# A list schedule of the MLP with other landing times, and six instead of four prepared weights ahead of its last part

## The chip, the cores and the metric

The kernel runs on one core of one Trainium2 chip. The metric is the device time of one execution in microseconds (us). The engines of the core are TensorE (PE; its weight loads are shown apart as PEld), VectorE (DVE), ScalarE (ACT), GpSimd (POOL) and SyncE (SP). SP issues plain transfers; POOL issues the transfers that add what they bring to what is there.

## The reference, cut to what matters

The model is an encoder of two layers on 512 tokens of width 1024. Each layer has a token part (attention, retention, gates) and a channel part, and the change is in the channel part alone:

```python
for i in range(DEPTH):
    ...
    x = layer_norm(DEEPNORM_ALPHA * x + y, ln1_g[i], ln1_b[i])
    ffn = conv_glu_ffn(x, w_up[i], conv_w[i], conv_b[i], w_down[i])
    ple = jax.nn.sigmoid(x @ w_ple_gate[i]) * (p[i] @ w_ple_proj[i])
    x = layer_norm(DEEPNORM_ALPHA * x + ffn + ple, ln2_g[i], ln2_b[i])

def conv_glu_ffn(x, w_up, conv_w, conv_b, w_down):
    h = x @ w_up
    hp = jnp.pad(h, ((0, 0), (1, 1), (0, 0)))
    h = hp[:, :-2] * conv_w[0] + hp[:, 1:-1] * conv_w[1] + hp[:, 2:] * conv_w[2] + conv_b
    a, b = jnp.split(h, 2, axis=-1)
    return (jax.nn.gelu(a) * b) @ w_down
```

Everything is float32. The up projection makes 2 x 2816 columns, the down projection takes 2816 back to 1024.

## The kernel before, in words

**Split operands.** A matmul here takes a float32 operand as a sum of a high part and a low part. ACT casts a weight to its high part (hi), DVE subtracts to get the low part (lo), and PE does three matmuls for each product (`mm3`: hi with hi, hi with lo, lo with hi). One weight is a tile of 128 x 1024, so it costs one load, one cast on ACT and one subtraction on DVE before PE can use it.

**Seven products for eight.** The larger matrix products are done block by block in seven products named a, c, t1, t2, d, t3 and t4, as in Strassen's scheme. Their weights are sums of blocks. Four of them are a chain in one buffer: a is loaded, split, then POOL adds a block to the same buffer (an accumulating transfer), which makes the raw t1; that is split, POOL adds again for t2, and again for t4. So t2's weights can't be split before t1's are, plus the time of the added transfer. t3 is a load and one added block; c and d are plain loads. Each product has two weights (j = 0 and 1).

**Segments.** The 22 row blocks of the hidden layer are cut into three segments of 3, 4 and 4 pairs (`SEGS`). For each segment an up part makes the hidden tiles and a down part multiplies them into the residual sum R. In the first segment the second weight of each down product is half as wide (512), since it has three pairs.

**What sets the order.** The engines run their instructions in the order in which the program issues them. Up to the first segment's up part, and again from the last down part on, that order comes from `Stream.get`, which prepares weights a few items ahead as it hands them out. In between, in `region` (lines 1615 to 1908), a list scheduler decides: `Plan` collects jobs for PE ("P"), ACT ("A"), DVE ("V"), POOL ("G") and SP ("S"), each with a duration from `COST`, the jobs it must follow, the buffers it takes and a due time. `dues` works the due times backwards from PE's fixed order. For a job with a transfer it subtracts the transfer and `COST["land"]`. `order` then plays the engines forward: whenever one is free it starts the most urgent job whose predecessors are done, whose buffers are free and whose due time is no further off than its `early`. A transfer counts as done at the end of a shared pipe plus `COST["land"]`. `run` does this for six settings (`PLANS`), keeps the one in which PE ends first, and issues the jobs in that order.

**Buffers in the plan.** `CAP` counts units ("u", 26), pairs for split weights ("w", 3), raw buffers ("r", 3), PSUM banks ("b") and temporaries ("t"). A weight with a pool of its own takes two units for its pair.

**The start of the region.** Some weights are already split there, some are only loaded or are being added to (`it.raw is not None`, line 1625). For the latter the plan holds their buffer and takes their data as landed at a fixed time, by `pl.past(6.0)` in line 1628. `TAIL` says when ACT and DVE are done with what was issued before (lines 217, 1867, 1896).

**The end of the region.** Lines 1877 to 1890 add the first four weights of the last down part (a and c, two each) to the plan, with due times counted from the plan's end `pl.now`, and the added blocks that follow them. Line 1905 then tells the stream that four weights are prepared. The last down part (from line 1912) takes them with `ws.get()`, which prepares t1, t2, d, t3 and t4 as it goes. At its first product the first layer also loads the next layer's input p (`ple_in`); the last layer loads the constants of the final norm (`ln_consts`).

The functions named in the steps below are `Stream.get` (534), `Plan.dues` (136), `Plan.order` (146) and `region` (1615) with `raw_of`, `plus` and `weights`.

Of the kernel before, what the change touches and what calls it, by code (L numbers as in the profile page):

```python
# [35 lines left out]
SEGS = (3, 4, 4)  # L36
# [36 lines left out]
DOWN = ("a", "c", "t1", "t2", "d", "t3", "t4")  # L73
CAP = {"u": 26, "w": 3, "r": 3, "b": 4, "t": 6}
COST = {"hi": 1.05, "lo": 1.22, "neg": 1.06, "centre": 0.79, "taps": 1.5, "gelu": 0.65, "mul": 0.69, "into": 0.69,
        "copy": 0.62, "issue": 1.0, "load": 1.45, "add": 3.0, "land": 3.0}
EARLY = {"w": 14, "g": 13, "s": 15, "c": 13, "d": 13, "t3": 14, "a": 28, "t1": 38, "t2": 30, "t4": 18}
AHEAD = 14

# [134 lines left out]
PLANS = ((1.0, 0), (0.9, 0), (0.8, 0), (1.0, 2), (0.6, 0), (1.2, 3))  # L214
SOON = 5
NEAR, SPARE = 10, 0
TAIL = (3.6, 4.3)
VG_HELD = (('0t1', '1t1', '0t2', '0c', '1t2', '1a', '1d', '1t3'), ('0a', '0c', '0t1', '1t1', '1t3', '1t2', '0t3', '0t2', '1d'))


# [42 lines left out]
def _f(a):  # L263
    return a.bitcast(F32)


def trunk(tc, wpack, x_nat, x_tr, head, p_tr, rpb, decay, ln_par, ln_col, conv, cos_t, sin_t, dist, xi_d, zd, mask, ident_d, out):
# [4 lines left out]
    with ExitStack() as es:  # L272
        pool = lambda name, bufs, **k: es.enter_context(tc.tile_pool(name=name, bufs=bufs, **k))
        cp = pool("const", 1)
        up = pool("unit", N_UNIT)
# [280 lines left out]
        ws = Stream()  # L556
# [261 lines left out]
        for l in range(DEPTH):  # L818
# [796 lines left out]
            def region():  # L1615

                pl = Plan(CAP)
                seq, at = ws.seq, [ws.nget]
                have, raws, ops, far = {}, {}, {}, []
                for it in seq[ws.nget:ws.nget + 40]:  # L1620
                    if it.hl is not None:
                        b = pl.held(*(("w", 1) if it.pool is None else ("u", 2)))
                        b.tile = it.hl
                        have[it] = b, None, None
                    elif it.raw is not None:
                        b = pl.held("r" if it.own is False or it.kind in "cdwgs" else "u")
                        b.tile = it.raw
                        raws[it] = b, pl.past(6.0)

                def raw_of(it):  # L1630

                    if it in raws:
                        return raws[it]
                    ll, c, o, w = it.src
                    raw = Buf(("u",) if it.own else ("r",), 1, lambda p: (up if p == "u" else rp).tile([P, 1024], F32, tag="u" if p == "u" else "raw", name=nm("raw")))
                    ok = pl.add("S", 0.1, lambda: nc.sync.dma_start(raw.tile[:, :w], wpack[ll, c][:, o:o + w]), takes=[raw],
                                dma=COST["load"] * w / 1024, early=EARLY[it.kind] - 4 + (AHEAD if it.plus else 0))
                    if it.plus is not None:
                        ok = plus(it, raw, [ok])
                    return raw, ok  # L1640

                def plus(it, raw, after):

                    ll, c, o, w = it.plus
                    return pl.add("G", COST["issue"], lambda: nc.gpsimd.dma_start(raw.tile[:, :w], wpack[ll, c][:, o:o + w], accum_op=ALU.add),
                                  after, uses=[raw], dma=COST["add"] * w / 1024)
# [4 lines left out]
                def weights(it, pools=None):  # L1651

                    if it in have:
                        return have[it]
                    hl = Buf(pools or (("u",) if it.kind in ("a", "t1", "t2", "s") else ("w", "u")), 2, pair)
                    if it.kind == "s":
                        ll, c, o, w = it.src
                        hi = pl.add("G", COST["issue"], lambda: nc.gpsimd.dma_start(hl.tile[0], wpack[ll, c]), takes=[hl], dma=COST["load"], early=EARLY["s"])
                        neg = pl.add("A", COST["neg"], lambda: nc.scalar.activation(hl.tile[1], _f(hl.tile[0]), AF.Copy, scale=-1.0), [hi], uses=[hl])
                        lo = pl.add("G", COST["issue"], lambda: nc.gpsimd.dma_start(hl.tile[1], wpack[ll, c], accum_op=ALU.add), [neg], uses=[hl], dma=COST["add"])  # L1660
                        have[it] = hl, hi, lo
                        return have[it]
                    raw, ok = raw_of(it)
                    cs, f = slice(0, it.width), it.width / 1024
                    hi = pl.add("A", COST["hi"] * f, lambda: nc.scalar.copy(hl.tile[0][:, cs], raw.tile[:, cs]), [ok], takes=[hl], uses=[raw], early=EARLY[it.kind])
                    lo = pl.add("V", COST["lo"] * f, lambda: nc.vector.tensor_sub(hl.tile[1][:, cs], raw.tile[:, cs], _f(hl.tile[0][:, cs])), [hi], uses=[raw, hl])
                    if it.nxt is not None:
                        raws[it.nxt] = raw, plus(it.nxt, raw, [hi, lo])
                    have[it] = hl, hi, lo
                    return have[it]  # L1670
# [192 lines left out]
                for p in range(SEGS[0]):  # L1863
                    halves[p // 2].tile = a11p[p // 2]
                    ops[0, p, 0] = halves[p // 2], (lambda p=p: a11[p]), []
                    b = pl.held("u")
                    ops[0, p, 1] = b, (lambda p=p: k2[p]), [pl.past(TAIL[1])] if p == p2 else []
                    for i in range(2):
# [4 lines left out]
                for s in range(1, len(SEGS)):  # L1873
                    up_part(s)
                    if s < len(SEGS) - 1:
                        down(s)
                s, nxt = len(SEGS) - 1, seq[at[0]:at[0] + 4]
                keep = []
                for i, it in enumerate(nxt):
                    hl, hi, lo = weights(it, ("w",) if it.pool is None else ("u",))  # L1880
                    lo.due = pl.now + 2.72 * i - 1
                    keep.append(hl)
                    hl.left += 1
                    if it.nxt is not None:
                        raws[it.nxt][0].left += 1
                        raws[it.nxt][1].due = pl.now + 2
                    if it.early is not None:
                        raws[it.early] = raw_of(it.early)
                        raws[it.early][0].left += 1
                        raws[it.early][1].due = pl.now + 6  # L1890
                for p in range(SEGS[s]):
                    for f, due in ((0, 0), (1, 5), (2, 10), (3, 10)):
                        b, _, js = ops[s, p, f]
                        b.left += 1
                        js[-1].due = min(js[-1].due, pl.now + due)
                pl.run({"A": TAIL[0], "V": TAIL[1]})
                for it in nxt:
# [4 lines left out]
                for p in range(SEGS[s]):  # L1902
                    a11[p], k2[p] = ops[s, p, 0][1](), ops[s, p, 1][1]()
                    sa[p], sb[p] = ops[s, p, 2][1](), ops[s, p, 3][1]()
                ws.nget, ws.nprep = at[0], at[0] + 4
                ws.nload = ws.nprep
                while seq[ws.nload].src is None or seq[ws.nload].kind == "t3":
                    ws.nload += 1

            region()  # L1910
            tile = NF
            for s in (len(SEGS) - 1,):
# [191 lines left out]
                for k in BOUND if not last else ("t4a", "t4b"):  # L2104
# [7 lines left out]
                    else:  # L2112
                        i = "ab".index(k[2]) + 2
# [143 lines left out]
```

## Time and profile before

| | us |
|---|---|
| median of three runs | 1678.01 |
| the three runs | 1676.4, 1678.01, 3372.79 |
| the profiled execution, its own time | 1676.4 |
| its span in the profile | 1674.6 |
| PE busy | 1659.7 |
| DVE busy | 1246.1 |
| ACT busy | 985.5 |
| POOL busy | 239.8 |

The run of 3372.79 us is far from the other two, and the comparisons leave it out.

In a row of the timeline stand the start in us, the duration, the engine, the line, the operation, the tile written and the tiles read, the shapes and the number of instructions in the row; in brackets stands how long the engine had been idle and what released it. Nearly all instructions of this part carry line 240, since a helper issues them, so the tile names have to tell them apart: `raw`, `rawa` and `rawt` are loaded weights (rawa a chain that starts with a, rawt t3), `hi` and `lo` are split weights, `u`, `v`, `w`, `x` and `gt` are PSUM banks, `sh` and `sl` the high and low part of the sums that t1, t2, d and t3 use, `k` the operand of c, `R` the residual. In the first layer the first down part begins on PE at 557.1 us of the span and the last one at 794.0; in the second layer the same places come about 832 us later.

### The profile page before, as it was taken

The numbers are of one execution on the slowest core, as the hardware profiler recorded it, in microseconds if no ns is written. First come the engines' busy times: TensorE is split into PE (matmuls) and PEld (weight loads), VectorE is DVE, ScalarE is ACT, GpSimd is POOL, SyncE is SP. The second block draws the span as 40 slices with busy tenths as digits, with TensorE's granted clock in tenths as the row PEclk, the third lists the DMA queues.
The fourth block names the chain that finished last, engine by engine and source line by source line (L and its number), as shares of the span: only waits on it lengthen the run. The fifth ranks groups of instructions, "written<-read, shape, count | busy, mean of one in ns | idle before, by whom it ended". The sixth has DMA issues, their size and how long they took to land.

```text
span 1674.6 us, 23525 instructions
## 1 busy us (share of the span) xinstructions
PE 1659.7 (99%) x8901; PEld 1433.9 (86%) x8901; DVE 1246.1 (74%) x1871; ACT 985.5 (59%) x1456; POOL 239.8 (14%) x280
## 2 busy tenths in 40 slices
PE   9999999999999999999999999999999999999997
PEld 7889988888888798898788899888888887988985
DVE  7766676777787769768876566877688887697687
ACT  6764676853367546356476647668534574563553
POOL 1111111110200112111112011111002011111113
PEclk9999999999999999999999999999999999999999
DMA  8989666676667778978689796667667777799684
GB/s 305 252 232 240 165 148 141 161 178 222 204 191 206 202 247 213 237 206 226 186 233 222 184 252 155 139 145 170 159 234 227 190 226 206 215 228 268 178 230 102
DMA packets 101362, 340.11 MB, mean 203 GB/s; under 512 B 11521, under 2 KB 16129, under 8 KB 101249
## 3 DMA queue, kind: packets, MB, share of 16 engines
q0 software_dynamic: 34128, 122.17, 39.6%
q1 hardware_dynamic: 67120, 216.44, 36.2%
q8 instruction: 70, 1.15, 0.3%
q14 instruction: 44, 0.35, 0.1%
HBM read 311.31 MB, written 25.69 MB: 201 GB/s over the span
## 4 chain that ended last, share of the span: by engine, by line
PE 81%; issue 13%; DMA 4%; DVE 1%; POOL 1%; ACT 0%; POOLq 0%; DVEq 0%; ACTq 0%
PE u L240 13%; PE gt L240 12%; PE v L240 7%; PE gt L560 6%; PE gt L561 6%; PE gt L562 6%; PE w L240 4%; PE gn L562 3%; PE gn L561 3%; PE gn L560 3%; DMA rawa<-in_wpack 2%; DMA raw<-in_wpack 2%; PE x L240 1%; PE u L560 1%; PE u L562 1%
## 5 line engine op out<-in xcount | busy, mean ns | idle before, releaser
L240 DVE TENSOR_TENSOR lo<-raw,hi 128x1024 fp32r<-128x1024 f32 (+1 forms) x189 | 224.5, 1209 | 74.2 <-ACT hi L240 73.4
L240 PE MATMUL gt<-x1t,hi 128*128 128x512 f32 x896 | 276.4, 390 | 0.0
L240 ACT CAST hi<-raw 128x1024 fp32r<-128x1024 f32 (+1 forms) x189 | 192.4, 1039 | 90.7 <-DMA raw<-in_wpack 74.6
L240 PEld LDWEIGHTS gt<-x1t,hi 128*128 128x128 f32 x896 | 166.7, 188 | 33.4
L240 PE MATMUL gt<-x1t,lo 128*128 128x512 f32 x448 | 174.5, 390 | 0.1
L240 POOL DMA_DIRECT2D raw<-in_wpack x64 | 55.5, 927 | 352.4 <-DVE lo L240 264.8
L240 DVE TENSOR_TENSOR lo<-rawa,hi 128x1024 fp32r<-128x1024 f32 x64 | 73.3, 1155 | 42.5 <-ACT hi L240 42.3
L560 PE MATMUL gt<-xt,hi 128*128 128x512 f32 x256 | 100.8, 394 | 0.0
L240 PEld LDWEIGHTS gt<-x1t,lo 128*128 128x128 f32 x448 | 84.1, 188 | 18.5 <-DVE lo L240 1.0
L561 PE MATMUL gt<-xt,hi 128*128 128x512 f32 x256 | 99.8, 390 | 0.0
L562 PE MATMUL gt<-xt,lo 128*128 128x512 f32 x256 | 99.7, 389 | 0.0
L320 ACT CAST hi<-raw 128x1024 fp32r<-128x1024 f32 x44 | 45.8, 1050 | 77.0 <-PE gt L561 31.3
L520 POOL DMA_DIRECT2D lo<-in_wpack x48 | 42.1, 876 | 296.2 <-ACT lo L519 219.6
L240 POOL DMA_DIRECT2D rawa<-in_wpack x48 | 43.7, 972 | 254.1 <-DVE lo L240 228.8
L518 ACT CAST hi<-raw 128x1024 fp32r<-128x1024 f32 x48 | 50.4, 1051 | 49.1 <-PE gt L561 41.2
L240 ACT CAST hi<-rawa 128x1024 fp32r<-128x1024 f32 x64 | 63.0, 998 | 26.9 <-DMA rawa<-in_wpack 19.9
L240 PE MATMUL v<-lo,sh 128*128 128x512 f32 x168 | 65.6, 390 | 1.7 <-DVE lo L240 1.7
L240 PE MATMUL v<-hi,sh 128*128 128x512 f32 x168 | 65.6, 390 | 1.0 <-ACT hi L240 1.0
L240 PE MATMUL v<-hi,sl 128*128 128x512 f32 x168 | 65.4, 389 | 0.0
L240 PE MATMUL u<-lo,sh 128*128 128x512 f32 x152 | 59.7, 393 | 1.9 <-DVE lo L240 1.8
L321 DVE TENSOR_TENSOR lo<-raw,hi 128x1024 fp32r<-128x1024 f32 x44 | 53.4, 1223 | 10.1 <-ACT hi L320 9.9
L240 PE MATMUL u<-hi,sh 128*128 128x512 f32 x152 | 59.2, 389 | 0.0
(394 smaller groups left out, 4869.5 us busy)
## 6 DMA issues: line engine op xcount, KB each, us to landing
raw<-in_wpack SPq DMA_DIRECT2D x235, 512.0 KB, 5.3
lo<-in_wpack POOLq DMA_DIRECT2D x64, 512.0 KB, 5.8
raw<-in_wpack POOLq DMA_DIRECT2D x64, 512.0 KB, 7.2
rawa<-in_wpack POOLq DMA_DIRECT2D x60, 512.0 KB, 7.4
sx<-s_scr SPq DMA_DIRECT2D x32, 512.0 KB, 8.5
rawa<-in_wpack SPq DMA_DIRECT2D x20, 512.0 KB, 6.7
rawt<-in_wpack SPq DMA_DIRECT2D x20, 512.0 KB, 6.8
rawt<-in_wpack POOLq DMA_DIRECT2D x20, 512.0 KB, 9.3
```

Source lines behind the costliest of these rows:

```text
L240: r = f(*a, **k)
L320: nc.scalar.copy(hi, src)
L321: nc.vector.tensor_sub(lo, src, _f(hi))
L518: nc.scalar.copy(hi[:, cs], it.raw[:, cs])
L520: nc.gpsimd.dma_start(lo[:, cs], wpack[l, c][:, o:o + w], accum_op=ALU.add)
L560: nc.tensor.matmul(ps, lh, rh, start=start, stop=False, skip_group_check=more)
L561: nc.tensor.matmul(ps, lh, rl, start=False, stop=False, skip_group_check=more)
L562: nc.tensor.matmul(ps, ll, rh, start=False, stop=stop, skip_group_check=more)
```

## The change

It changes three things in the planner and leaves the computation and the transfers as they are.

- A transfer counts as landing 4.2 us after the pipe instead of 3.0, in the due times and in the forward play alike.
- At the region's start ACT and DVE count as free from 4.2 and 4.9 us instead of 3.6 and 4.3, and pending raw data counts as landed at once (0.0), that of t2 at 7.5 us, instead of 6.0 for all.
- Six instead of four weights of the last down part go into the plan: both of t1 as well. Their splits are due five us ahead of their use instead of one, the added blocks that make t2 of them are due 9 us after the plan's end, and the sixth weight, t1's second, gets its pair from the units. The stream is told of six.

```diff
-        "copy": 0.62, "issue": 1.0, "load": 1.45, "add": 3.0, "land": 3.0}
+        "copy": 0.62, "issue": 1.0, "load": 1.45, "add": 3.0, "land": 4.2}
...
-TAIL = (3.6, 4.3)
+TAIL = (4.2, 4.9)
+LANDED = {"t2": 7.5}
...
-                        raws[it] = b, pl.past(6.0)
+                        raws[it] = b, pl.past(LANDED.get(it.kind, 0.0))
...
-                s, nxt = len(SEGS) - 1, seq[at[0]:at[0] + 4]
+                s, nxt = len(SEGS) - 1, seq[at[0]:at[0] + 6]
                 keep = []
                 for i, it in enumerate(nxt):
+                    if i == 5:
+                        it.pool = up
                     hl, hi, lo = weights(it, ("w",) if it.pool is None else ("u",))
-                    lo.due = pl.now + 2.72 * i - 1
+                    lo.due = pl.now + 2.72 * i - (1 if i < 4 else 5)
                     keep.append(hl)
                     hl.left += 1
                     if it.nxt is not None:
                         raws[it.nxt][0].left += 1
-                        raws[it.nxt][1].due = pl.now + 2
+                        raws[it.nxt][1].due = pl.now + (2 if i < 4 else 9)
...
-                ws.nget, ws.nprep = at[0], at[0] + 4
+                ws.nget, ws.nprep = at[0], at[0] + 6
```

## The prediction

> **What bounds the kernel now.** I read the busy table first, then the time by stage, then the waits of TensorE (PE), then the timeline of each engine around the places where PE waits.
>
> ```profile
> span 1674.6 us, 23525 instructions
> ## 1 busy us (share of the span) xinstructions
> PE 1659.7 (99%) x8901; PEld 1433.9 (86%) x8901; DVE 1246.1 (74%) x1871; ACT 985.5 (59%) x1456; POOL 239.8 (14%) x280
> ```
>
> PE is busy all the time but 1674.6 - 1659.7 = 14.9 us, and the change takes no matmul away. So whatever it brings must come out of these 14.9 us. The time by stage shows where they are; its columns are the stretch, its length, and busy time with instruction count of each engine, then the clock of PE, the DMA share and GB/s.
>
> ```profile
> 560.00:570.00 10.00, 10.00 (x46) 8.29 (x45) 9.19 (x14) 6.57 (x9) 1.73 (x2) 1.00 0.57 128
> 570.00:580.00 10.00, 8.58 (x35) 6.20 (x35) 6.62 (x9) 2.19 (x3) 2.62 (x3) 1.00 1.06 302
> 810.00:820.00 10.00, 9.00 (x39) 6.78 (x38) 9.93 (x12) 6.01 (x6) 1.71 (x2) 1.00 0.72 119
> 1400.00:1410.00 10.00, 8.84 (x38) 6.68 (x36) 8.56 (x11) 2.26 (x4) 3.45 (x4) 1.00 1.05 310
> 1640.00:1650.00 10.00, 9.10 (x39) 6.88 (x38) 8.84 (x11) 7.86 (x9) 1.72 (x2) 1.00 0.75 119
> 1660.00:1670.00 10.00, 5.65 (x24) 4.32 (x24) 8.56 (x15) 4.41 (x8) 9.72 (x9) 0.90 0.53 132
> ```
>
> An undisturbed stretch holds 46 matmuls in 10 us: one each 0.227 us (three rows below, 568.01, 568.24, 568.47, show it). Four stretches fall short: two in each layer, at the same place of it. One is in the first down part (570 and 1400), one in the last (810 and 1640). The row of 1660 is the drain after the matmuls. The granted clock is 1.00 in all four, so waiting alone costs there. The waits name the releasers:
>
> ```profile
> PE u L240 <- DVE lo L240: 1.8, 3, 0.8
> PE v L240 <- DVE lo L240: 1.7, 2, 0.8
> PE warm L667 <- DVE warm L664: 1.2, 1, 1.2
> PE v L240 <- ACT hi L240: 1.0, 2, 0.6
> ```
>
> Apart from the warm-up every wait is for a split weight (hi from ACT, lo from DVE), and all belong to the products t2 (u) and d (v) of these down parts. The idle time of 4.5 us understates the loss, since a modelled matmul lasts 0.39 us while 0.227 apart; counted in missing matmuls it is 11 + 7 + 8 + 7 = 33 of 0.227, or 7.5 us, give or take one per stretch. Over the starts themselves I get 7.0 (the first stall alone: 577.25 - 576.28 and 578.60 - 577.25, less 0.227 each, are 1.87).
>
> **First stall: the order in which ACT and DVE take the weights.**
>
> ```profile
> 576.28 0.39 PE L240 MATMUL v<-hi,sa 128*128 128x512 f32 x1
> 577.25 0.50 PE L240 MATMUL v<-hi,sh 128*128 128x512 f32 x1 [0.58 <-ACT hi L240]
> 578.60 0.50 PE L240 MATMUL v<-lo,sh 128*128 128x512 f32 x1 [0.84 <-DVE lo L240]
> ```
> ```profile
> 575.62 1.05 ACT L240 CAST hi<-rawa 128x1024 fp32r<-128x1024 f32 x1 [3.92 <-DMA rawa<-in_wpack]
> 576.58 0.61 ACT L240 CAST hi<-raw 128x512 fp32r<-128x512 f32 x1
> ```
> ```profile
> 576.71 1.22 DVE L240 TENSOR_TENSOR lo<-rawa,hi 128x1024 fp32r<-128x1024 f32 x1 [0.76 <-ACT hi L240]
> 577.85 0.69 DVE L240 TENSOR_TENSOR lo<-raw,hi 128x512 fp32r<-128x512 f32 x1
> ```
> ```profile
> 568.00 0.86 POOL L240 DMA_DIRECT2D rawa<-in_wpack  x1 [2.01 <-DVE lo L240]
> ```
> ```profile
> 550.66 0.33 SPq L240 DMA_DIRECT2D raw<-in_wpack  x1
> ```
>
> PE wants the second weight of product d (512 wide, "d1") at 576.5. ACT casts it only at 576.58, because ahead of it in ACT's order stands t4's first weight, for which ACT waits 3.92 us: its accumulating transfer left POOL at 568.00 and landed 7.5 us later. d1's own load left SP at 550.66, so its data was not what was late.
>
> Why the planner chose that order follows from the code. It takes d's and t2's pending data as landed at 6.0 alike, lets t2's split go first, and believes a buffer of kind r free for d1 only after the split of d's first weight. So it dates d1's landing after that of t4's sum. With the change I walked through the list by hand. The load of d's first weight ends at 0.1 + 1.45 + 4.2 = 5.75, t2's sum counts as landed at 7.5, and ACT and DVE so take d's weight ahead of t2's. d1's load then starts at 9.95 and lands at 10.05 + 0.73 + 4.2 = 15.0; t4's sum is issued at 12.45 and lands at 12.45 + 1.0 + 3.0 + 4.2 = 20.65. So d1 is cast well ahead of t4, and both parts of the stall go: 11 and 8 missing matmuls, up to 4.3 us in the two layers.
>
> The price lies on DVE, where d's first split (1.13 us, the pitch of the rows 565.35 and 566.48) now comes before two urgent ones.
>
> ```profile
> 565.35 1.22 DVE L240 TENSOR_TENSOR sl<-ss,sh 128x1024 fp32r<-128x1024 f32 x1
> 566.48 1.22 DVE L240 TENSOR_TENSOR lo<-rawa,hi 128x1024 fp32r<-128x1024 f32 x1
> ```
> ```profile
> 568.01 0.39 PE L240 MATMUL v<-hi,sh 128*128 128x512 f32 x1
> 568.24 0.39 PE L240 MATMUL v<-lo,sh 128*128 128x512 f32 x1
> 568.47 0.39 PE L240 MATMUL v<-hi,sl 128*128 128x512 f32 x1
> ```
>
> sl would end at 565.35 + 1.22 + 1.13 = 567.7, used at 568.47; t2's split at 568.8, used five steps after 568.47, at 569.6. Each keeps 0.75 us. If that cover is gone, the loss is the excess over 0.75; I allow 0.5 us for both layers. t4's add leaves POOL 1.1 us later (569.1) and lands near 576.6; t4 comes after d1's 6 and t3's 18 matmuls, so not before 576.5 + 24 x 0.227 = 582. t1's second weight no longer waits for the sums of the last up tile, so t2's second add leaves POOL earlier than before. ACT's and DVE's later start in the plan (4.2 and 4.9) only delays what the planner believes; what runs is the order.
>
> **Later landing elsewhere.** Every plain load counts 1.2 us later, so its due time is 1.2 us earlier, and the chains a, t1, t2, t4 gain 1.2 per link. Instruction counts stay, SP and POOL issue the same transfers in nearly the same order. Between 590 and 794 PE never waits, so there is nothing to gain, and what may be lost is bounded by the slack. The tightest weight I found there:
>
> ```profile
> 734.58 1.23 DVE L240 TENSOR_TENSOR lo<-raw,hi 128x1024 fp32r<-128x1024 f32 x1 [0.52 <-ACT hi L240]
> ```
> ```profile
> 738.74 0.39 PE L240 MATMUL gt<-x1t,lo 128*128 128x512 f32 x1
> ```
>
> It is done at 735.8 and first used at 738.74: 2.9 us, more than one cast and one split (1.05 + 1.22) put ahead of it. I cost this edit at 0, with 2 us per layer as the upper end.
>
> The medians of issue to landing tell which constant is nearer the chip:
>
> ```profile
> raw<-in_wpack SPq DMA_DIRECT2D x235, 512.0 KB, 5.3
> lo<-in_wpack POOLq DMA_DIRECT2D x64, 512.0 KB, 5.8
> raw<-in_wpack POOLq DMA_DIRECT2D x64, 512.0 KB, 7.2
> rawa<-in_wpack POOLq DMA_DIRECT2D x60, 512.0 KB, 7.4
> ```
>
> The planner has 0.1 + 1.45 + land for a load (4.55 before, 5.75 after, 5.3 measured) and 1.0 + 3.0 + land for an add (7.0, 8.2; 7.4 measured). The old figures were short of the chip, the new ones are not, so I go by the rows and count the lead as needed. The Trainium skill, page "DMA: Bandwidth & Descriptors", section "Anatomy of one DMA — SWDGE (gpsimd) path", fits a transfer issued by POOL as 2.0 us and its bytes at 436 GB/s, an estimate of 3.2 us for 512 KB. By that page even the old figure would be long, more lead would be idle, and the time would stay at 1676.4; the trace does not agree (5.8 to 7.4 us).
>
> **Second stall: six weights instead of four.**
>
> ```profile
> 801.45 1.22 DVE L240 TENSOR_TENSOR lo<-raw,hi 128x1024 fp32r<-128x1024 f32 x1
> ```
> ```profile
> 803.12 1.83 POOL L240 DMA_DIRECT2D raw<-in_wpack  x2 [24.80 <-DVE lo L240]
> ```
> ```profile
> 808.64 1.05 ACT L240 CAST hi<-raw 128x1024 fp32r<-128x1024 f32 x1 [5.43 <-DMA raw<-in_wpack]
> ```
> ```profile
> 813.51 1.21 DVE L240 TENSOR_TENSOR lo<-raw,hi 128x1024 fp32r<-128x1024 f32 x1
> ```
> ```profile
> 810.35 0.39 PE L240 MATMUL u<-hi,sh 128*128 128x512 f32 x1
> ```
>
> t2 starts at 810.35 and lacks its first lo (split after the cast of 808.64) and then its second (813.51, behind sums and statistics of c). Both come from adds that leave POOL at 803.12, when t1 has been split at 801.45. POOL had idled 24.80 us. With t1's two splits in the plan, DVE takes them in slots between the last up tile's steps, one of them this:
>
> ```profile
> 793.00 1.23 DVE L240 TENSOR_TENSOR lo<-raw,hi 128x1024 fp32r<-128x1024 f32 x1 [1.70 <-ACT hi L240]
> ```
>
> By the list I get splits near 789 and 792, adds 10 to 12 us earlier. The bound from the other side is their due times, 5.88 and 7.78 after the part's start at 794.0: end of the first at 801.1 instead of 802.7. Even then the cast of 808.64 comes 1.6 us sooner and t2's first split ends near 809.3, before its use at 810.58. And the second now stands ahead of c's sums: the weight t1_1 leaves one of three w pairs free, so the fetch of c's first weight already prepares t2's second. So both waits go at either end: 7 and 7 matmuls, 3.2 us.
>
> What is hidden: 2 casts and 2 splits (2 x 1.05, 2 x 1.22) only change places; t2's split now stands ahead of the sum of a on DVE, which frees t2's bank; the sum moves by no more than t1's two splits (from 801.45 on), which are gone from there. On SP the next layer's input load stands behind two more unit buffers:
>
> ```profile
> 794.04 0.33 SPq L240 DMA_DIRECT2D pst<-in_p_tr  x1
> ```
>
> **Sum.** 7.5 (all 33 matmuls) less 0.5 = 7.0 us. The profiled execution took 1676.4 with a span of 1674.6; it gives 1669.4. The median shown, 1678.0, stands 1.6 above it and would give 1671.0. I predict the middle, 1670.2.
>
> **Rivals.**
>
> Only one stall goes, or a new wait of 3 us takes the place of one. For it: the two margins of 0.75 us. Against: the order argument holds for any landing between 4 and 12 us. Time: 1670.2 + 3.3 = 1673.5.
>
> The change does nothing: the orders come out as before, or the transfers land within the old lead, so that no split is late for want of it. Against: ACT's waits of 3.92 and 5.43 us for transfers. Time: 1677, the middle of 1676.4 and 1678.0. (The page named above would have it so.)
>
> Slower: the unit pool runs short. t1_1's pair sits on two units from about 790 to 810. The load of 794.04 then waits for the next units, which a's end frees at 794.04 + 24 x 0.227 = 799.5; d's loads queue behind it on SP, and t2's second cast stands behind its cast on ACT. That decides from a landing past 810, thus if units come free only when t1 ends (810.3): landing at 815, splits near 818 instead of 813.5, 5 us more in each layer (in the second, the loads of the norm constants stand in that place). Time: 1670.2 + 10 = 1680. Against: a landing of 4 to 5 us after 799.5 is 804.
>
> **Numbers.** Both stalls go: 0.66 (own range 1667.5 to 1672.5). One: 0.18. Nothing: 0.07. Slower: 0.09. The range 1667 to 1677 leaves out the slower case and some of the noise. Two per cent, about what a measurement of this kernel can tell from no change, are 33 us: more than twice all of PE's idle time, so faster by that is excluded but for 0.01; slower by that would need ten lost weights in each layer, 0.02; the same 0.97.
>
> **What would show it.** Right: the stretches of 570, 810, 1400 and 1640 hold 46 matmuls; a 512-wide cast stands ahead of the 1024-wide one that waits near 571 to 577; two POOL adds leave between 787 and 800 and POOL's idle time of 24.80 is cut. Wrong: a new row among PE's waits, above all for sl or t2 near 568 to 570, or SP waiting for units after 794.

## The result, and the profile after

| | before | after |
|---|---|---|
| median, us | 1678.01 | 1669.13 |
| runs, us | 1676.4 to 1680.16 | 1668.86 to 1669.32 |
| the profiled execution, us | 1676.4 | 1669.08 |
| its span, us | 1674.6 | 1667.0 |

The ratio is 0.9949, with a 95% interval of 0.9933 to 0.9964: half a per cent faster. That is far less than the two per cent of which the prediction speaks, but the interval is narrow enough to tell it from no change. Three single runs of 2361 to 3373 us are left out of all ratios and ranges, but the medians given count them (without the one of 3372.79 us, 1678.01 would be 1677.2).

The busy table of the changed kernel:

```profile
span 1667.0 us, 23550 instructions
## 1 busy us (share of the span) xinstructions
PE 1657.2 (99%) x8901; PEld 1435.2 (86%) x8901; DVE 1243.8 (75%) x1871; ACT 986.1 (59%) x1456; POOL 239.8 (14%) x280
```

The same 8901 matmuls; PE is idle for 1667.0 - 1657.2 = 9.8 us instead of 14.9. The four stretches that fell short (length, then PE's busy time and matmuls first, granted clock third from the end), and all of PE's waits that are left:

```profile
570.00:580.00 10.00, 10.00 (x46) 8.29 (x45) 7.67 (x12) 1.05 (x1) 3.18 (x4) 1.00 0.98 276
810.00:820.00 10.00, 10.00 (x46) 8.29 (x45) 8.20 (x10) 5.29 (x6) 0.00 (x0) 1.00 0.52 173
1400.00:1410.00 10.00, 10.00 (x46) 8.29 (x45) 6.63 (x9) 1.27 (x2) 2.02 (x3) 1.00 1.03 272
1640.00:1650.00 10.00, 10.00 (x46) 8.29 (x45) 9.28 (x13) 5.60 (x8) 0.55 (x1) 1.00 0.01 2
```
```profile
PE warm L668 <- DVE warm L665: 1.2, 1, 1.2
```

All four are full and no wait has come in their place. The lines of the code stand one further down, since the change adds one. In this execution the first down part begins 0.6 us later than before, at 557.71, and the last 1.8 us earlier, at 792.27. ACT in the first down part, where it used to cast t4's first weight ahead of d's second:

```profile
568.10 0.62 ACT L241 CAST hi<-rawa 128x512 fp32r<-128x512 f32 x1 [0.30 <-DMA rawa<-in_wpack]
569.11 0.62 ACT L241 CAST hi<-raw 128x512 fp32r<-128x512 f32 x1 [0.39 <-PE v L241]
578.66 1.05 ACT L241 CAST hi<-rawa 128x1024 fp32r<-128x1024 f32 x1 [8.93 <-DMA rawa<-in_wpack]
581.41 0.62 ACT L241 CAST hi<-rawa 128x512 fp32r<-128x512 f32 x1 [1.69 <-DMA rawa<-in_wpack]
581.93 1.05 ACT L241 CAST hi<-raw 128x1024 fp32r<-128x1024 f32 x1
```

d's second weight (128x512 from raw) is cast at 569.11, 7.5 us earlier, and the wait for t4's sum stands behind it. That wait is longer than before, 8.93 us instead of 3.92, and costs nothing: nobody urgent is queued behind it. An engine's idle time alone tells little; what stands behind it in the engine's order decides. POOL ahead of the last down part:

```profile
784.20 0.85 POOL L241 DMA_DIRECT2D raw<-in_wpack  x1 [8.96 <-DVE cb L241]
792.09 0.85 POOL L241 DMA_DIRECT2D raw<-in_wpack  x1 [7.04 <-DVE lo L241]
```

These are t2's two adds. They left together at 803.12 before, after 24.80 us of idleness.

### The profile page after: what moved, and what is told of

Same layout as the page of the kernel before. It is cut to its first block, busy times and chain, and to the rows that moved or that the text cites. A ratio compares the mean times of both kernels' runs of the same rounds, so it can differ in the third digit from the quotient of the medians.

```text
span 1667.0 us, 23550 instructions
## 1 busy us (share of the span) xinstructions
PE 1657.2 (99%) x8901; PEld 1435.2 (86%) x8901; DVE 1243.8 (75%) x1871; ACT 986.1 (59%) x1456; POOL 239.8 (14%) x280
## 4 chain that ended last, share of the span: by engine, by line
PE 99%; DVE 1%; ACT 0%; POOL 0%; issue 0%; DVEq 0%; POOLq 0%; ACTq 0%
PE gt L241 21%; PE u L241 19%; PE v L241 10%; PE gt L561 6%; PE gt L562 6%; PE gt L563 6%; PE w L241 5%; PE gn L562 3%; PE gn L563 3%; PE gn L561 3%; PE x L241 1%; PE u L561 1%; PE u L563 1%; PE u L562 1%; PE gn L241 1%; PE na L1188 1%
```

## The experiments

All stand beside runs of the kernel before on the same chip; "ratio" is to those, with its 95% interval. The first two runs take one down part each.

**Six weights alone.** The kernel before with the third part of the change only.

```diff
-                s, nxt = len(SEGS) - 1, seq[at[0]:at[0] + 4]
+                s, nxt = len(SEGS) - 1, seq[at[0]:at[0] + 6]
...
-                    lo.due = pl.now + 2.72 * i - 1
+                    lo.due = pl.now + 2.72 * i - (1 if i < 4 else 5)
...
```

> The kernel before with six instead of four weights in the plan and nothing else (land 3.0, pending data at 6.0, TAIL as before). My theory: the two stalls have separate causes, and six weights repair only the last down part. 810:820 and 1640:1650 hold 46 matmuls instead of 39, 570:580 and 1400:1410 stay at 35 and 38; t2's adds leave POOL near 784 and 792 instead of 803. Gain 14 matmuls of 0.227, 3.2 us: 1673.2 against 1676.4. Rival (the later landing is what starts every transfer earlier, and six weights alone come too late): gain under 1 us, and a wait for u stays in the last down part.

Measured: 1673.38 against 1676.93, ratio 0.9978 (0.9969 to 0.9986), thus 3.6 us. Its stretches:

```profile
570.00:580.00 10.00, 8.56 (x36) 6.22 (x35) 7.46 (x10) 2.19 (x3) 2.62 (x3) 1.00 1.06 305
...
810.00:820.00 10.00, 10.00 (x45) 8.27 (x45) 8.90 (x12) 4.36 (x5) 0.32 (x1) 1.00 0.71 210
...
1400.00:1410.00 10.00, 8.46 (x35) 6.14 (x34) 7.72 (x10) 2.19 (x3) 2.69 (x4) 1.00 1.06 305
...
1640.00:1650.00 10.00, 10.00 (x46) 8.28 (x45) 5.97 (x8) 4.99 (x6) 0.00 (x0) 1.00 0.55 113
```

The last down part is repaired, the first isn't touched. The two stalls are separate, and six weights repair theirs without any later landing.

**One pair swapped.** The kernel before, with the finished order changed by hand at one place and every constant as it was.

```diff
         assert end < 1e9
+        for e in "AV":
+            w = lambda kind, width: next(i for i, (j, _) in enumerate(order) if j.eng == e and j.it and (j.it.kind, j.it.width) == (kind, width))
+            late, first = w("d", 512), w("t4", 1024)
...
+            order.insert(first, order.pop(late))
         for j, pools in order:
...
+                    hi.it = lo.it = it
```

The last line marks each cast and split with its weight, so that the swap can find it.

> The kernel before with every constant as it was; in the finished order only the cast and the split of d's second weight (512 wide) are moved ahead of those of t4's first weight. My theory (order): this alone repairs the first down part: 570:580 and 1400:1410 hold 45 or 46 matmuls instead of 35 and 38, no wait for v is left there; 810 and 1640 stay at 39. Gain 1.9 us per layer by the starts, 3.7 to 4.3 us in all: about 1672.4 against 1676.4. Rival (lead): the first stall went because transfers are planned, and so issued, with more lead; no transfer moves here, so the stall stays: 1676.4, gain under 0.5 us.

Measured: 1675.69 against 1676.93, ratio 0.9988 (0.9979 to 0.9997): 1.2 us, neither the 4 nor the nothing. PE's waits and the two stretches of the first down parts, then the place of the new wait on DVE and PE:

```profile
PE gt L245 <- DVE lo L245: 2.2, 2, 1.2
PE u L245 <- DVE lo L245: 1.6, 3, 0.7
```
```profile
570.00:580.00 10.00, 10.00 (x44) 7.90 (x43) 6.99 (x10) 2.20 (x3) 2.62 (x3) 1.00 1.06 301
...
1400.00:1410.00 10.00, 10.00 (x45) 7.88 (x44) 8.03 (x11) 2.20 (x3) 3.00 (x4) 1.00 1.05 299
```
```profile
589.61 1.22 DVE L245 TENSOR_TENSOR lo<-raw,hi 128x1024 fp32r<-128x1024 f32 x1
```
```profile
590.88 0.50 PE L245 MATMUL gt<-x1t,lo 128*128 128x512 f32 x1 [1.01 <-DVE lo L245]
```

The waits for v are gone, as the order theory has it, and a wait for gt has come, some 13 us later: the first weight of the next up part (g). In ACT's order it stands behind t1 of the next block, and t1's added transfer lands later than before. ACT's casts of t1 and g, in the kernel before and in this one:

```profile
582.45 2.00 ACT L240 CAST hi<-raw 128x1024 fp32r<-128x1024 f32 x2 [1.73 <-DMA raw<-in_wpack]
```
```profile
584.99 2.00 ACT L245 CAST hi<-raw 128x1024 fp32r<-128x1024 f32 x2 [3.81 <-DMA raw<-in_wpack]
```

So the stall had covered a second one. My theory was right about the mechanism and too small: one pair isn't all that the changed plan moves. It also has g ahead of t1; that is the cast at 581.93 above.

**Two pairs swapped.** The same, with g ahead of t1 as well.

```diff
-            late, first = w("d", 512), w("t4", 1024)
...
-            order.insert(first, order.pop(late))
+            for late, first in ((("d", 512), ("t4", 1024)), (("g", 1024), ("t1", 1024))):
+                late, first = w(*late), w(*first)
...
+                order.insert(first, order.pop(late))
```

> The kernel before, all constants as they were, with two pairs swapped in the finished order on ACT and DVE: d's second weight ahead of t4's first (as in the run before), and the first weight of the next up part (g) ahead of the next block's t1. With the first swap alone 1.18 and 1.39 us of the 3.7 us came back as a wait for that weight g, whose cast stood behind t1's late added transfer; the changed kernel's plan has g ahead of t1. My theory (order, now of two pairs): no wait is left from 570 to 794, the last down part stays at 39 of 46: 1673.2 against 1676.9, gain 3.7. Rival (the later landing is needed as well, the waits only move on): gain 1.2 us as with one swap, and a new wait between 580 and 610.

Measured: 1673.71 against 1676.71, ratio 0.9980 (0.9971 to 0.9989): 3.0 us of the 3.7. The wait for g is gone, but not every wait, as the theory had it: a smaller one has come some 10 us further on (at 600.36), for the tile gg that DVE works on:

```profile
PE u L246 <- DVE lo L246: 1.5, 2, 0.8
PE warm L673 <- DVE warm L670: 1.2, 1, 1.2
PE gt L246 <- DVE gg L246: 0.9, 2, 0.5
```

**Two pairs and six weights,** with land, the pending dates and `TAIL` as before.

> The two swaps and six weights, every other constant as before (land 3.0, pending data at 6.0, TAIL 3.6 and 4.3). My theory: these two pairs and the two weights are all of the change that the time sees. 1669.1 to 1670.0, within 1 us of the changed kernel, no wait of PE but the warm-up. Rival (later landing is worth something of its own): 1671 or more, with waits elsewhere.

Measured: 1669.93 against 1676.71, ratio 0.9956 (0.9943 to 0.9968). The time lies at the upper edge of the range: 6.8 us come from two pairs and two weights. But they are not quite all that the time sees. In the same series the runs below with five weights and with the pending dates and six weights took 1668.57 and 1668.33, and the slowest of them (1668.88) is faster than the fastest here (1669.62). Three waits of 0.2 us are left, which the changed kernel doesn't have. Two of them stand at t2's second weight in the second layer:

```profile
1401.33 0.50 PE L246 MATMUL u<-hi,sh 128*128 128x512 f32 x1 [0.17 <-ACT hi L246]
1402.05 0.50 PE L246 MATMUL u<-lo,sh 128*128 128x512 f32 x1 [0.22 <-DVE lo L246]
```

Counted over the starts (1400.77 ahead of them, 1402.39 behind), these two cost 0.33 + 0.49 + 0.11 = 0.9 us, and the one for gg some 0.4. That makes 1.3 of the 1.4 to 1.6 us that are missing. The pending dates move more in the order than the two pairs.

**The pending dates with and without TAIL.** Land 3.0 and four weights in both. They differ only in whether the planner counts ACT and DVE as free at 3.6 and 4.3 or at 4.2 and 4.9.

```diff
-TAIL = (3.6, 4.3)
+TAIL = (4.2, 4.9)
...
-                        raws[it] = b, pl.past(6.0)
+                        raws[it] = b, pl.past({"t2": 7.5}.get(it.kind, 0.0))
```

> Only the pending data (landed at once, t2 at 7.5) and TAIL (4.2, 4.9) of the change; land stays at 3.0, four weights. The plan then still has t4's first weight ahead of d's second on ACT and DVE. My theory: the first stall stays (570:580 and 1400:1410 short by 8 to 11 matmuls), the last too; only t2's second add leaves POOL some half a us earlier, which is worth 0.15 us per layer. 1676 against 1676.4, gain under 0.7 us. Rival (the pending data's own dates are what repairs the first down part): 1672.4.

> As the run with pending data and TAIL, but TAIL stays at (3.6, 4.3): it differs from it by 0.6 us in when the planner counts ACT and DVE as free, and by nothing else. The plan then has d's first weight ahead of t2's first, its second load earlier, and its second weight ahead of t4's first. My theory (order): the first stall goes, 570:580 and 1400:1410 hold 45 or 46, the last stays (39): 1672.4 against 1676.4, gain 3.7 to 4.3 us. Rival (lead): land is 3.0 as before, no transfer is given more lead, so this run and its twin agree within 0.5 us.

Measured: with TAIL 1674.86, ratio 0.9983 (0.9974 to 0.9992), without 1671.57, ratio 0.9964 (0.9951 to 0.9976). ACT in the first down part, with and without:

```profile
574.29 1.05 ACT L240 CAST hi<-rawa 128x1024 fp32r<-128x1024 f32 x1 [4.13 <-DMA rawa<-in_wpack]
575.25 0.62 ACT L240 CAST hi<-raw 128x512 fp32r<-128x512 f32 x1
```
```profile
570.07 0.62 ACT L240 CAST hi<-raw 128x512 fp32r<-128x512 f32 x1
576.89 1.05 ACT L240 CAST hi<-rawa 128x1024 fp32r<-128x1024 f32 x1 [6.20 <-DMA rawa<-in_wpack]
```

Six tenths of a microsecond in what the planner believes turn the two casts round (and put d's first weight ahead of t2's, as expected), and that is 3.3 us. The transfers' lead is the same in both, so the lead isn't what pays. Both gained more than I expected. With TAIL, t4's sum of the first layer landed 1.3 us sooner than before (cast at 574.29 against 575.62, from adds that left POOL at 567.90 and 568.00), so half of that stall went without the two casts changing places. The add took 6.3 us from issue to landing instead of 7.5, and the load that had left SP at 570.48 left at 572.39; that the one follows from the other is not shown. In both runs the last down part gained too, 41 matmuls instead of 39 in 810:820 and 1640:1650; by the starts it is 0.3 us in the first layer. There t2's adds left POOL 8.7 us after the start of the part instead of 9.1; why DVE came to t1's splits sooner I did not find out.

**Landing later alone.** Land 4.2, all else as before.

> The kernel before with land 4.2 and nothing else. Its plan has d's second weight ahead of t4's first, but the next block's t1 ahead of t4's second and of g. My theory (order): the waits for v go (3.7 us), a wait for gt or for t4's second weight comes in their place as in the run with one swap (2.6 us), the last down part stays at 39 of 46: 1675.6 against 1676.8, between 1674 and 1677. Rival (the landing time is the part that pays): 1672.5 to 1673.

Measured: 1676.17 against 1677.08, ratio 0.9992 (0.9983 to 1.0001), which is no change that the runs can tell. PE's waits:

```profile
PE u L240 <- DVE lo L240: 3.8, 5, 1.1
PE warm L667 <- DVE warm L664: 1.2, 1, 1.2
PE x L240 <- DVE lo L240: 0.4, 2, 0.2
PE x L240 <- ACT hi L240: 0.2, 1, 0.2
```

The waits for v are gone and others took their place, but not at gt: t2's second split now stands behind t3's second and the next a on DVE (u), and t4's second cast behind t1's (x).

**Landing still later.** The changed kernel with land 6.6.

```diff
-        "copy": 0.62, "issue": 1.0, "load": 1.45, "add": 3.0, "land": 4.2}
+        "copy": 0.62, "issue": 1.0, "load": 1.45, "add": 3.0, "land": 6.6}
```

> The changed kernel with land 6.6 instead of 4.2: still more lead for every transfer. Its plan has t4's first weight ahead of d's second again, t2's second split behind t3's and the next a's, and the next up part's first weight g behind t1 and another a. My theory (what counts is the order that comes out, not the lead): the waits for v return (1.9 us per layer) and one for gt comes (1 to 3 us per layer): 1675 to 1680 against 1669.1. Rival (lead is what helps, and more of it does no harm): 1669 to 1670.

Measured: 1682.98 against 1677.08, ratio 1.0036 (1.0023 to 1.0049), slower than the kernel before, and worse than the order theory had it.

```profile
PE v L241 <- ACT hi L241: 4.3, 2, 2.2
PE v L241 <- DVE lo L241: 2.5, 4, 0.8
PE u L241 <- DVE lo L241: 1.4, 2, 0.7
```
```profile
570.00:580.00 10.00, 7.10 (x29) 4.99 (x27) 6.12 (x8) 1.56 (x2) 2.62 (x3) 1.00 1.02 274
580.00:590.00 10.00, 9.16 (x33) 7.45 (x34) 6.58 (x11) 3.67 (x4) 0.86 (x1) 0.83 1.06 319
```

The wait for v came back, because t4 stands ahead of d again; the one for gt that I expected did not, t2's second weight (u) did. Some 4 us of the excess are the clock, told below. More lead is not better; it makes another order, and this one is bad.

**Five weights instead of six.**

```diff
-                s, nxt = len(SEGS) - 1, seq[at[0]:at[0] + 6]
+                s, nxt = len(SEGS) - 1, seq[at[0]:at[0] + 5]
...
-                ws.nget, ws.nprep = at[0], at[0] + 6
+                ws.nget, ws.nprep = at[0], at[0] + 5
```

> The changed kernel with five weights instead of six in the plan: only t1's first weight is split inside it. My theory (each of t2's two weights waits for its own added transfer, which leaves when its t1 has been split): the first wait of t2 (0.42 us) goes, the second (0.9 us, once per layer) stays: 1669.1 + 1.8 = 1670.9. Rival (the two waits are one, and go with the first add; or the second t1 weight is split early enough by the stream anyway): 1669.1 to 1669.5.

Measured: 1668.57 against 1676.71, ratio 0.9949 (0.9935 to 0.9962): my theory fell, the rival's number is met. POOL shows that t2's second add leaves late all the same:

```profile
783.51 0.86 POOL L241 DMA_DIRECT2D raw<-in_wpack  x1 [8.96 <-DVE cb L241]
801.83 0.86 POOL L241 DMA_DIRECT2D raw<-in_wpack  x1 [17.46 <-DVE lo L241]
```

Its split stands on DVE at 808.42 and ends at 809.65, before its use at 810.84. In the kernel before, DVE had stood idle for t2's first split until 809.72, with the sums and statistics of c queued behind it and t2's second split behind those, at 813.51. With the first split early, c's sums run at 804.99 and the second is in time. The second add also lands sooner now that it leaves alone: it is cast 5.5 us after it left POOL (807.34), against about 7 us for the second of the two that left together (811.24). No run parts the two effects, but repairing the first wait repairs both: in that sense the two waits were one.

**The least of it.** First the pending dates and six weights, without land and without TAIL; then the same with five weights, beside the changed kernel itself.

> The change without its landing time and without TAIL: land stays at 3.0, TAIL at (3.6, 4.3); only the pending data's dates and the six weights. Its plan has d's second weight ahead of t4's first and g ahead of t1, as the changed kernel's has. My theory: same orders at the two places, same time: 1669.4 within 0.7 us of 1669.1. Rival (landing as later is the part that pays): a wait remains, 1671 or more.

> The changed kernel itself once more, beside the others of this call: 1669.1 by every theory, within 0.5 us.

> The least of the change that should bring all of it: the pending data's dates (at once, t2 at 7.5) and five weights instead of six; land 3.0 and TAIL as before. My theory: no wait of PE but the warm-up is left, so 1668.3 to 1669.1, not below the changed kernel by more than 1 us, since nothing but the start and the drain is left to gain. Rival (land, TAIL or the sixth weight pay for something the single runs did not show): 1670 or more.

Measured: 1668.33 against 1676.71, ratio 0.9947 (0.9933 to 0.9960); and in another series 1668.44, ratio 0.9943 (0.9928 to 0.9958), beside 1668.61, ratio 0.9945 (0.9929 to 0.9962), for the changed kernel. All three have no wait of PE but the warm-up. The landing time, TAIL and the sixth weight can stay away. None of these versions is faster than the changed kernel by more than the spread.

## Why the prediction was right, point by point

- **What bounds.** Right in the count: the span lost 7.6 us, against 7.5 counted in missing matmuls. But "whatever it brings must come out of these 14.9 us" was too strict. Idle time fell by 5.1 us (14.9 to 9.8) and busy time by 2.5 (1659.7 to 1657.2) for the same 8901 matmuls, since the table books 0.39 us for a matmul that nothing follows at once, and 0.50 for the one after a wait, where 0.227 is the pitch.
- **The walk through the list.** Right in its order: ACT and DVE run as it said. Its margins were met: sl ends at 567.05 + 1.22 = 568.27 and t2's split at 569.41, used at 569.04 and 570.17:

```profile
567.05 1.22 DVE L241 TENSOR_TENSOR sl<-ss,sh 128x1024 fp32r<-128x1024 f32 x1
568.19 1.22 DVE L241 TENSOR_TENSOR lo<-rawa,hi 128x1024 fp32r<-128x1024 f32 x1
```
```profile
569.04 0.39 PE L241 MATMUL v<-hi,sl 128*128 128x512 f32 x1
...
570.17 0.39 PE L241 MATMUL u<-lo,sb 128*128 128x512 f32 x1
```

  0.77 and 0.76 us are left of the 0.75 said, and the 0.5 us allowed for a loss there weren't needed.
- **t4.** Its add left POOL at 569.70, which is 569.1 on the clock of before, as said. It was cast at 578.66, as soon as it had landed; 576.6 was said, 577.2 on this clock, so it came some 1.5 us later. t4's lo is done at 579.75 + 1.23 = 581.0 and first used at 582.41: 1.4 us were left, less than I had thought.
- **The first stall as one pair.** The step "So d1 is cast well ahead of t4, and both parts of the stall go" was too short. The one swap brought 1.2 us of the expected 4. Behind the stall I took slack from the trace as it stood. The weight g was split and used there as follows:

```profile
587.07 1.22 DVE L240 TENSOR_TENSOR lo<-raw,hi 128x1024 fp32r<-128x1024 f32 x1
```
```profile
591.38 0.39 PE L240 MATMUL gt<-x1t,lo 128*128 128x512 f32 x1
```

  That is 591.38 - 588.29 = 3.1 us, more than the tightest that I named (2.9). But PE would come 1.9 us earlier, and ACT's cast came 2.5 later (584.99 for 582.45): 3.1 - 1.9 - 2.5 = -1.3, and a wait of 1.0 to 1.2 us it was. The sum still held, because the new plan also puts g ahead of t1, to which I had not walked. That part was luck.
- **Later landing elsewhere at 0.** Right: without land and TAIL the time is the same (1668.33). But "I go by the rows and count the lead as needed" was wrong. Constants nearer to the measured landings were not needed. A later landing alone brought 0.9 us, with an interval that reaches past no change, and 6.6 in the changed kernel made it 5.9 us slower than the kernel before.
- **ACT's and DVE's later start.** That it "only delays what the planner believes; what runs is the order" was wrong as a reason to put it at nothing: the belief makes the order. With the pending dates alone the first stall goes (1671.57); with TAIL beside them and land 3.0 it stays in good part (1674.86). The changed kernel has these dates and this TAIL with land 4.2, and the stall is gone (six weights alone leave it as it was). So the later landing is not idle in the change: it makes up for TAIL, and without TAIL neither is needed.
- **The second stall.** Right in size: 3.2 said, 3.6 measured alone. t1's splits stand on DVE at 782.29 and 790.58, on the clock of before 784.1 and 792.3; near 789 and 792 was said, so the second came where it was expected and the first earlier still. That six were needed, one for each of t2's weights, was wrong; five do. With six, t2's second split does stand ahead of c's sums, as said (804.61 and 805.75 on DVE); with five it stands behind them and is in time all the same.
- **The load of pst behind the units.** It left SP at 797.90, on the clock of before 799.7; 799.5 was said. No wait for units came, so the slower rival had no start.
- **The sum.** 7.0 was said against the profiled execution's 1676.4, and 7.3 came (1669.08). The profile's number was the better base than the median of three runs: over 27 later runs the kernel before has a median of 1676.93.

## What to carry to other kernels

In a list schedule, read a cost constant by the orders that it turns round, not by how near it is to the chip: swap the pair by hand, with all constants as they were, to see what it is worth. Behind a stall that goes, walk on to the next weights on the same engines, with PE earlier by what was won; their slack in the old trace includes the stall. Two waits close together on an in-order engine may be one: repair the first and look again.

## What the runs showed of the hardware

**A transfer that starts earlier can make another land later.** With one pair swapped, d's raw buffer came free earlier, and two loads left SP at 576.91 instead of 578.57, close behind two adds that POOL had issued at 575.91 (575.59 before). The two adds of that moment, in the kernel before and in this one (KB each, median us from issue to landing):

```profile
raw<-in_wpack POOLq DMA_DIRECT2D x2, 512.0 KB, 8.7
```
```profile
raw<-in_wpack POOLq DMA_DIRECT2D x2, 512.0 KB, 10.6
```

They took 1.9 us longer. That is the landing that t1's cast, and g behind it, waited for. With two pairs swapped the loads left 1.0 us behind the adds again (576.29 and 575.29), and the adds took 10.6 us again. That the loads caused it is argued from their order in time; no run took the loads alone away.

**Short stalls can cost the clock.** In the profiled execution of six weights alone, the matmuls after the first stall of the second layer ran at half pace; the same place of the kernel before did not. Columns as in the stretches above, first six weights, then before:

```profile
1405.00:1410.00 5.00, 3.47 (x15) 2.34 (x14) 3.90 (x5) 1.56 (x2) 1.74 (x2) 1.00 1.04 351
1410.00:1415.00 5.00, 5.00 (x16) 3.93 (x16) 1.89 (x3) 0.83 (x2) 0.00 (x0) 0.66 1.07 238
```
```profile
1405.00:1410.00 5.00, 3.84 (x16) 2.63 (x14) 4.46 (x6) 1.57 (x2) 2.04 (x3) 1.00 1.02 347
1410.00:1415.00 5.00, 4.90 (x22) 4.05 (x23) 1.47 (x4) 0.62 (x1) 0.00 (x0) 1.00 1.07 232
```

After two gaps of 1.07 and 1.35 us between starts, with one matmul in between, eight matmuls came 0.42 us apart, 3.4 us in all: 8 x (0.424 - 0.227) = 1.6 us lost. That execution took 1675.32, the longest of its eleven. Gaps of 0.81 and 1.34 at the same place of the kernel before left the clock at 1.00, and so did those of the first layer in both executions (0.97 and 1.35 before, 0.95 and 1.33 with six weights). With land 6.6, where one gap was 2.6 us, both layers lost clock (0.83 in 580 to 590, 0.73 in 1410 to 1420), and eight and twelve matmuls 0.43 apart cost 4.0 us. The Trainium skill, page "TensorE: Matmul & The Clock Gate", section "What's actually happening", has the clock at half after an idle window of about 3.4 us, with windows that run free of the program. The slow stretch of 3.4 us agrees with such a window (the twelve matmuls with land 6.6 take 5.1 us, longer than one); but here gaps that are together shorter than a window, with work between them, were enough at one of the four stalls of these two executions.

It may be why the kernel before spreads over 1676.02 to 1680.55 us and the changed one, which has no such gap, over 1668.27 to 1669.32. The time does go with the mean granted clock: among 55 executions of the kernel before, the 13 with 0.999 took 1676.06 to 1676.93 us, the 31 with 0.998 took 1676.02 to 1679.35, the nine with 0.997 took 1677.93 to 1679.00, and the two with 0.996 took 1680.05 and 1680.55. That the stalls are what lowers it no run tested. It would also explain why the changed kernel gains more against the median (8.5 us in the last series) than the 7.5 us of missing matmuls.
